# Interleaved steps of gate, up and down in a one-layer decoder, both PSUM pools shared, two step orders rewritten

## The chip, the cores and the metric

The kernel runs on one core of one Trainium2 chip. A time is the device time of one execution in microseconds (us); the median of several runs is given, and one execution was taken with the hardware profiler. The engines are named as in the profile: PE (TensorE, matrix products), PEld (its weight loads), DVE (VectorE), ACT (ScalarE), POOL (GpSimd) and SP (the queue that issues most transfers).

## What is computed

One inference step of a one-layer decoder on 1024 prompt tokens and 32 sample tokens (8 sequences of 4), 1056 tokens in all, width 1024. The layer has a combined input projection that feeds four head groups (sliding-window attention, a gated linear recurrence, a short convolution and a pooling mixer), an output projection, cross-attention into 256 memory tokens and a SwiGLU feed-forward part of hidden width 2816, each followed by a layer norm. Cut to the part that matters:

```python
mix = jnp.concatenate([o_a, o_b, o_c, o_d], axis=-1) @ w_o
x = layer_norm(ALPHA * x + mix, ln1_g, ln1_b)
x = layer_norm(ALPHA * x + memory_attention(x, mem_k, mem_v, w_xq, w_xo), ln2_g, ln2_b)
ffn = (jax.nn.silu(x @ w_gate) * (x @ w_up)) @ w_down
x = layer_norm(ALPHA * x + ffn, ln3_g, ln3_b)
```

## The kernel before

Everything is 32-bit. A matrix product in full accuracy is made of three: each operand is split into a rounded high part and a rest (`split`, line 202: a cast on ACT, line 203, and a subtraction, line 211, mostly on DVE), and `mm3` (line 194) adds high by high (line 196), high by rest (197) and rest by high (199).

PSUM has eight banks, in two pools: `PM` (line 139, tag `pm`) has three and `PSB` (line 143, tag `psb`) has five. Before, the products of the big projections, of gate and of up take `PM`; the second product of the feed-forward part, transposes and small products take `PSB`.

The work is written as Python generators, each of which stops at every `yield`; a string with one letter for each step says in which order the generators are resumed (`play`, line 1018; when the string ends, all generators are run out). A letter whose generator has ended does nothing. `ORDER1` (line 36) orders the first part: input norm (I), values (V), memory (M), columns of the input projection (T), window attention (S), the two recurrences (A, B), pooling (P). `ORDER2` (line 37) orders the second: splits of the mixed heads by token chunk (X), output projection (W), norms (N, nine steps each, in the order of `NORMS`), one cross-attention line for each of four token chunks (0 to 3, beginning with two steps of the query projection) and the first pairs of the feed-forward part (F). `ORDER3` is not used before; the order of the last part stands in `CFG`.

What is written is a preference: the library (`schedule_with_timeline_sim=True`, line 1847) settles at build time in which order each engine takes its instructions, and places the semaphores. Each engine then works through its own fixed queue.

The feed-forward part has 22 tiles of 128 hidden columns, taken in pairs p. The first pairs (p below 4) run in the second part and just behind it (`ff_early`). The rest runs in two halves of the tokens (`hf` 0: tokens 0 to 511; `hf` 1: 512 to 1055). For each pair there are three steps. `half_gate` and `half_up` (1669, 1681) call `products` (1623): it loads two weight tiles, makes sums and differences of their quarters (`sc`, `s4`, lines 1634 to 1637, in the tile `work`), splits them, and runs seven products of 12 matmuls each instead of eight, a scheme after Strassen and Winograd; the results are added up by DVE (lines 1649, 1673, 1697). Gate ends with silu; up multiplies by it (1698) and splits the product into `hh` (lines 1693 and 1694). `half_down` (1708) is the second product: it loads two weight tiles, splits them, and runs 16 steps of 6 matmuls, each of which DVE adds to the running sum `M` (1727; 1725 in the first pair of the second half).

The loop of the first half (1786) writes gate of pair p, down of pair p-1, up of pair p, each whole. The loop of the second half (1802) does the same, with one half of `finish` (1738: output norm of a block of 128 tokens, transposed by PE at line 217, then DVE, ACT, POOL and a store) after gate and one after down; there are four such blocks. In the last pair down of p-1 follows up of p. At the very end `play` runs the last down with the five remaining `finish`.

Of the kernel before, what the change touches and what calls it, by code (L numbers as in the profile page):

```python
# [19 lines left out]
KD = D // P  # L20
# [6 lines left out]
NF = DFF // P  # L27
# [5 lines left out]
LEVELS = (32, 16, 8, 4)  # L33
CFG = {'early': [[0, [0]], [0, [1]], [1, [0, 1]], [2, [0, 1]]], 'fin': {0: 0, 1: 1, 2: 1, 3: 1, 6: 1, 7: 1, 8: 1, 4: 0}, 'fpm': 1, 'VG': 'VVV', 'acc': 'VVV', 'xl': 'VVVV', 'mul': 'VVVV', 'zs': 'VVV', 'ai': 0, 'px': 'V', 'wo': [[0], [1], [2], [3]], 'ls': 384, 'rs': 3, 'sub': 'VVVV', 'sq2': 99, 'dn': 0, 'early2': [[3, [0, 1]]], 'order3': 'dddddddd87dddd8877dddd56dddddddd5566'}
NORMS = [(0, 2), (1, 2), (0, 4), (2, 2), (1, 4), (3, 2), (2, 4), (3, 4)]
ORDER1 = "MMIMMIIIIIVIVIIVCMMIIIVIIVVTIMTVVVTTTTTTTSTSTSTSTSTSTTTTSSAAASAATTAAAATTTTTAAAAAAATATTSSASSTTTTTTBBTTBBBBABBTTTTTTBBBBTTTBBBBBBBBTTTTTBBBTTBTTBPTBBBTTBTTPT"
ORDER2 = "XXWXXWWWWWWWNWXNWWWNNWNXWNNNWNWN00XW00NWNNWWNNN0NN0WWW0WW00W00WNWN1NNN1W11NNNNWWW1NWW11NNNFF11NNNNFF1N1N22NNNNNN22NNFFNNFNF2FFN2NF22N2NFNFN223NNFN33F3N33FNFNFFNF3N333FN3FF3F33F3F33333333FFFFNNFNNFNNFNNNFNF"
ORDER3 = "aaPPPPPPPPPPPPPPPPPPPPPPPPPbaabbbAAAAAvdvddvvdBBBBCCCCBCwccwwccxwxDDDxxDDxyEExyEEEzz"

# [49 lines left out]
def build(ctx: ExitStack, tc: tile.TileContext, A):  # L89
# [139 lines left out]
    flags = set()  # L229
# [787 lines left out]

    def play(order, streams):
        order = order.replace(" ", "")

        for a in order:
            run(streams[a], 1)
        for g in streams.values():
            run(g, 999)

# [516 lines left out]
    need("n4.0", "n4.256", "n4.512", "n4.768")  # L1542

# [75 lines left out]
    g3t = []  # L1621

    def products(hf, src, p, result):
# [17 lines left out]
        g4 = split(s4, w4[:, 0], w4[:, 1], V)  # L1641

        def prod(w, k0, x):
            ps = PM(n)
            mm3(ps, lambda k: w[0][:, k0 + k, :], lambda k: w[1][:, k0 + k, :], x[0], x[1], 4)
            return ps

        def add(o, ps, y):
            V.tensor_tensor(o, ps, y, ALU.add)

        S.copy(sn[:, 0], prod(g1, 0, B11))
        result(0, prod(g1, 4, B21), sn[:, 0], sn[:, 2])
# [52 lines left out]

    hx = {}

    def half_down(hf, p, order=None):
# [8 lines left out]
        flat = [tuple(t.rearrange("p c n -> p (c n)") for t in x) for x in hs]  # L1717
        for f, (t0, t1) in order or [(f, r) for f in range(KD) for r in PART[hf]]:
            ps = PSB()[:, :t1 - t0]
            fs = slice(f * P, f * P + P)  # L1720
            mm3(ps, lambda k: d[k][0][:, fs], lambda k: d[k][1][:, fs], lambda k: flat[k][0][:, t0 - o:t1 - o],
                lambda k: flat[k][1][:, t0 - o:t1 - o], 2)
            z = M[:, f, t0:t1]
            if hf and not p:
                V.scalar_tensor_tensor(z, z, ALPHA, ps, ALU.mult, ALU.add)
            else:
                V.tensor_tensor(z, z, ps, ALU.add)  # L1727
            yield
# [47 lines left out]

    NP = NF // 2
    tk = []
    EA = max(p for p, _ in CFG["early2"]) + 1
    t1 = sums_a(tk)  # L1780
# [70 lines left out]
```

## Time and profile before

| | us |
|---|---|
| median of 3 runs | 1448.58 |
| lowest, highest run | 1447.52, 1449.3 |
| the profiled execution's own time | 1450.38 |
| its span, first to last instruction | 1448.6 |
| PE busy in it (matmuls) | 1350.5 (93%) |
| DVE busy | 1084.1 (75%) |
| ACT busy | 656.7 (45%) |
| POOL busy | 239.6 (17%) |

The profile comes from the execution of 1450.38 us. A row of instructions gives start, length, engine, line, operation, the tile written and the tiles read (buffer numbers left out), and in square brackets how long the engine was idle before it and what ended that. PE's matmuls are pipelined: one of 256 columns is shown with 0.28 us, while the next starts some 0.12 us later. Waits are given as engine, line waiting, what it waited for, us in total, times, longest. In a table by stretch, each engine has its busy time and the number of its instructions, and PEclk is the granted clock of PE as a share of full speed.

### The profile page before, as it was taken

The numbers are of one execution on the slowest core, as the hardware profiler recorded it, in microseconds if no ns is written. First come the engines' busy times: TensorE is split into PE (matmuls) and PEld (weight loads), VectorE is DVE, ScalarE is ACT, GpSimd is POOL, SyncE is SP. The second block draws the span as 40 slices with busy tenths as digits, with TensorE's granted clock in tenths as the row PEclk, the third lists the DMA queues.
The fourth block names the chain that finished last, engine by engine and source line by source line (L and its number), as shares of the span: only waits on it lengthen the run. The fifth ranks groups of instructions, "written<-read, shape, count | busy, mean of one in ns | idle before, by whom it ended". The sixth has DMA issues, their size and how long they took to land.

```text
span 1448.6 us, 25150 instructions
## 1 busy us (share of the span) xinstructions
PE 1350.5 (93%) x10065; PEld 1279.5 (88%) x10065; DVE 1084.1 (75%) x1972; ACT 656.7 (45%) x1134; POOL 239.6 (17%) x164
## 2 busy tenths in 40 slices
PE   6999999998998997689988999999998999999995
PEld 5998888996897996589788999999998989999995
DVE  5814569588657768686575989988599988888877
ACT  4424662432655767575455434343343444333341
POOL 4322453365000001012042000000400000000001
PEclk8999999999898999699999999999999999999998
DMA  8201102111253435152411333332233333232321
GB/s 297 69 24 44 31 15 63 47 39 34 79 150 113 135 114 146 30 144 91 144 59 59 102 117 88 102 103 88 74 110 109 114 90 118 88 102 81 95 88 62
DMA packets 188446, 132.61 MB, mean 92 GB/s; under 512 B 14572, under 2 KB 177617, under 8 KB 188305
## 3 DMA queue, kind: packets, MB, share of 16 engines
q1 hardware_dynamic: 187225, 128.27, 29.6%
q0 software_dynamic: 928, 2.67, 0.6%
q8 instruction: 79, 1.29, 0.4%
q14 instruction: 38, 0.31, 0.1%
q10 hardware_dynamic: 176, 0.07, 0.0%
HBM read 125.32 MB, written 6.78 MB: 91 GB/s over the span
## 4 chain that ended last, share of the span: by engine, by line
PE 67%; DVE 17%; ACT 7%; DMA 4%; issue 3%; SPq 1%; POOL 1%; DVEq 0%; ACTq 0%; POOLq 0%
PE pm L196 14%; PE pm L197 14%; PE pm L199 14%; PE ps L196 5%; PE ps L199 5%; PE ps L197 5%; DVE wl L211 3%; PE ps L217 2%; ACT M L157 2%; ACT wh L203 1%; DMA rw<-in_w_down 1%; DMA rw<-in_w_up 1%; DVE R L458 1%; PE ps L625 1%; PE pm L1072 1%
## 5 line engine op out<-in xcount | busy, mean ns | idle before, releaser
L196 PE MATMUL pm<-Xh,wh 128*128 128x256 f32 (+3 forms) x1240 | 350.3, 306 | 20.9 <-ACT Xh L1130 6.3
L197 PE MATMUL pm<-Xl,wh 128*128 128x256 f32 (+3 forms) x1240 | 347.9, 304 | 2.3 <-DVE Xl L948 1.5
L196 PEld LDWEIGHTS pm<-Xh,wh 128*128 128x128 f32 x1240 | 238.3, 193 | 30.2 <-ACT Xh L1130 9.6
L197 PEld LDWEIGHTS pm<-Xl,wh 128*128 128x128 f32 x1240 | 238.4, 192 | 6.1 <-DVE Xl L1131 2.0
L203 ACT CAST wh<-rw 128x1024 fp32r<-128x1024 f32 x145 | 151.9, 1050 | 132.1 <-PE pm L197 77.8
L199 PE MATMUL pm<-Xh,wl 128*128 128x256 f32 (+3 forms) x1240 | 206.8, 299 | 2.2 <-DVE wl L211 2.2
L199 PEld LDWEIGHTS pm<-Xh,wl 128*128 128x128 f32 x1240 | 179.7, 189 | 4.3 <-DVE wl L211 2.6
L211 DVE TENSOR_TENSOR wl<-rw,wh 128x1024 fp32r<-128x1024 f32 x122 | 155.0, 1273 | 33.9 <-ACT wh L203 29.4
L197 PE MATMUL ps<-hh,dh 128*128 128x272 f32 (+3 forms) x592 | 152.5, 285 | 1.6 <-DVE hh L1694 1.6
L196 PE MATMUL ps<-hh,dh 128*128 128x272 f32 (+3 forms) x592 | 144.8, 287 | 5.1 <-ACT hh L1693 4.8
L1727 DVE TENSOR_TENSOR M<-M,ps 128x272 f32<-128x272 f32 (+3 forms) x280 | 107.2, 415 | 28.9 <-PE ps L199 28.0
L199 PE MATMUL ps<-hh,dl 128*128 128x272 f32 (+3 forms) x592 | 118.6, 284 | 0.0
L196 PEld LDWEIGHTS ps<-hh,dh 128*128 128x128 f32 x592 | 105.4, 189 | 7.0 <-ACT hh L1693 6.1
L197 PEld LDWEIGHTS ps<-hh,dh 128*128 128x128 f32 x592 | 108.8, 189 | 2.7 <-DVE hh L1694 2.7
L211 POOL TENSOR_TENSOR wl<-rw,wh 128x1024 fp32r<-128x1024 f32 x23 | 58.2, 2530 | 292.7 <-ACT wh L203 273.4
L199 PEld LDWEIGHTS ps<-hh,dl 128*128 128x128 f32 x592 | 92.0, 188 | 0.0
L203 ACT CAST dh<-rw 128x1024 fp32r<-128x1024 f32 x44 | 45.5, 1050 | 101.2 <-PE ps L197 45.6
L203 ACT CAST g<-work 128x1024 fp32r<-128x1024 f32 x34 | 35.6, 1048 | 72.0 <-PE pm L197 48.5
L196 PE MATMUL pm<-mixh,wh 128*128 128x256 f32 (+1 forms) x256 | 66.0, 292 | 0.0
L197 PE MATMUL pm<-mixl,wh 128*128 128x256 f32 (+1 forms) x256 | 65.6, 290 | 0.2 <-DVE mixl L1165 0.2
L196 PE MATMUL pm<-Xh,g 128*128 128x272 f32 (+1 forms) x216 | 56.7, 291 | 4.7 <-ACT g L203 3.0
L211 POOL TENSOR_TENSOR dl<-rw,dh 128x1024 fp32r<-128x1024 f32 x8 | 19.7, 2458 | 244.3 <-PE ps L217 200.8
(437 smaller groups left out, 3045.6 us busy)
## 6 DMA issues: line engine op xcount, KB each, us to landing
rw<-in_w_gate SPq DMA_DIRECT2D x45, 512.0 KB
rw<-in_w_up SPq DMA_DIRECT2D x44, 512.0 KB
rw<-in_w_down SPq DMA_DIRECT2D x44, 512.0 KB
rw<-in_w_o SPq DMA_DIRECT2D x23, 384.0 KB
rw<-in_w_in SPq DMA_DIRECT2D x15, 512.0 KB
xraw<-in_x_prompt SPq DMA_DIRECT2D x8, 512.0 KB
out_y_prompt<-y SPq DMA_DIRECT2D x8, 512.0 KB
vreg<-in_w_o SPq DMA_DIRECT2D x9, 384.0 KB
```

The source lines that it names most:

```text
L157: i = S.activation(out, in_, func, **kw)
L196: PE.matmul(out, wh(k), xh(k), start=(start and k == 0), stop=False)
L197: PE.matmul(out, wh(k), xl(k), start=False, stop=False)
L199: i = PE.matmul(out, wl(k), xh(k), start=False, stop=(k == nk - 1))
L203: S.copy(hi, raw)
L211: (e or G).tensor_tensor(lo, raw, hi.bitcast(F32), ALU.subtract)
L217: PE.transpose(out, in_, ident[:n, :n])
L458: V.tensor_tensor(r5, g5[:, :, :, 1, :], q5[:, :, :, 1, :], ALU.mult)
L625: PE.matmul(ps[:, g * 256:g * 256 + nk], M[js, g, q0:q0 + P], kT[js, k0:k0 + nk], start=True, stop=True)
L1072: PE.matmul(ps, identr, x[:, f, t0:t1], start=first, stop=False)
L1727: V.tensor_tensor(z, z, ps, ALU.add)
```

## The change

`products` now stops (`yield`) before the first product and after nearly every product, and takes its bank from either pool after the pattern MBMBMBB (M for `PM`, B for `PSB`). `half_down` stops once its weights are loaded and split, and takes its banks after the pattern BMBBMBBM. Both loops of the feed-forward part call `play` with a string for each pair: `ORDER4` for the first half, `ORDER5` for the second with `finish` as f, which is not run out at the end of a pair (the new argument `keep`), and `ORDER6` for the last pairs. `half_up` asserts at build time that down of the pair before has been written. `ORDER1` and `ORDER2` are other strings with the same letters. The former `order3` of `CFG` is now `ORDER3`, with one more d in front for the new stop.

The words that came with the change also say that the weight sums of gate get own buffers. The diff has no such edit: `sc` and `s4` stay in `work`.

```diff
-ORDER1 = "MMIMMIIIIIVIVIIVCMMIIIVIIVVTIMTVVVTTTTTTTSTSTSTSTSTSTTTTSSAAASAATTAAAATTTTTAAAAAAATATTSSASSTTTTTTBBTTBBBBABBTTTTTTBBBBTTTBBBBBBBBTTTTTBBBTTBTTBPTBBBTTBTTPT"
-ORDER2 = "XXWXXWWWWWWWNWXNWWWNNWNXWNNNWNWN00XW00NWNNWWNNN0NN0WWW0WW00W00WNWN1NNN1W11NNNNWWW1NWW11NNNFF11NNNNFF1N1N22NNNNNN22NNFFNNFNF2FFN2NF22N2NFNFN223NNFN33F3N33FNFNFFNF3N333FN3FF3F33F3F33333333FFFFNNFNNFNNFNNNFNF"
+ORDER1 = "MIMMIIIMIIVIVIIIVCMMIMIVVVTTIIIVVVTTTTTTTSTSSTTSTSTSTTTTSAAASSATATAAAATTTTTAAAATAAATATSSASTTTTTTSBBTTTBBTTABBBBBBBTTTBTTTBBBBTBBBBBBBBTTTTPTTTTBBBBBPTTTTTT"
+ORDER2 = "XXWWXXWWXWWWWWNNWWWNNWNXNNNWNWWN00NXNNNNW0WWW0NWN00WW0WW00W00WNNWN1NNN1W11NNNWWW1NNF1F1NNN11NNNNF1WW1FNNNNNNNN2222NNFF22NNNNFNNF2FF2FN2FFNN2F233NN3FNF33FNFFNFN33N3N3F3N3F3FF33F33F33333FN3F3FFFNFFFFNNNNNNNN"
+ORDER3 = "ddddddddd87dddd8877dddd56dddddddd5566"
+ORDER4 = "gggdggddggddggddddddddddddduuuuuuuuu"
+ORDER5 = "gggdggddggddggddddfddddddddduuuufuuuuu"
+ORDER6 = "gggggggggduuuuuuuuuddddddddddddddddd"
...
         def prod(w, k0, x):
-            ps = PM(n)
+            ps = PM(n) if next(turn) == "M" else PSB()[:, :n]
...
+        yield
         S.copy(sn[:, 0], prod(g1, 0, B11))
+        yield
         result(0, prod(g1, 4, B21), sn[:, 0], sn[:, 2])
+        yield
         ps = prod(g3, 4, T2)
         add(sn[:, 0], ps, sn[:, 0])
         yield
         ps = prod(g2, 0, T3)
         add(sn[:, 1], ps, sn[:, 0])
+        yield
         ps = prod(g3, 0, T1)
         add(sn[:, 0], ps, sn[:, 0])
         result(3, ps, sn[:, 1], sn[:, 2])
+        yield
         result(1, prod(g4, 0, B22), sn[:, 0], sn[:, 0])
+        yield
         result(2, prod(g2, 4, T4), sn[:, 1], sn[:, 1])
         yield
...
-        for f, (t0, t1) in order or [(f, r) for f in range(KD) for r in PART[hf]]:
-            ps = PSB()[:, :t1 - t0]
+        yield
+        for i, (f, (t0, t1)) in enumerate(order or [(f, r) for f in range(KD) for r in PART[hf]]):
+            ps = PM(t1 - t0) if "BMBBMBBM"[i % 8] == "M" else PSB()[:, :t1 - t0]
...
     for p in range(EA, NP):
-        run(half_gate(0, p), 99)
-        if p > EA:
-            run(half_down(0, p - 1), 99)
-        run(half_up(0, p), 99)
+        play(ORDER4, {"g": half_gate(0, p), "d": half_down(0, p - 1) if p > EA else none(), "u": half_up(0, p)})
...
-    for p in range(1, NP):
-        run(half_gate(1, p), 99)
-        run(fa, 1)
-        if p < NP - 1:
-            run(half_down(1, p - 1), 99)
-        run(fa, 1)
-        if p == 5:
+    for p in range(1, NP - 1):
+        play(ORDER5, {"g": half_gate(1, p), "d": half_down(1, p - 1), "f": fa, "u": half_up(1, p)}, "f")
+        if p == 4:
             run(fa, 99)
             free(*gbs)
-        run(half_up(1, p), 99)
-        if p == NP - 1:
-            free(*g3t)
-            run(half_down(1, p - 1), 99)
+    play(ORDER6, {"g": half_gate(1, p + 1), "u": half_up(1, p + 1), "d": half_down(1, p)})
+    free(*g3t)
```

## Rows read from the trace of the kernel before

**Rows 1.** The page's slices: PE's busy tenths in 40 equal parts.

```profile
PE   6999999998998997689988999999998999999995
```

**Rows 2.** Busy time by stage: stretch, length, engines with counts, granted clock, DMA.

```profile
0.00:390.00 390.00, 366.78 (x2310) 331.64 (x2311) 245.22 (x440) 162.92 (x323) 150.13 (x110) 0.96 0.23 69
390.00:825.00 435.00, 393.10 (x2992) 363.23 (x2991) 309.19 (x515) 255.57 (x497) 53.70 (x32) 0.95 0.36 105
825.00:1020.00 195.00, 191.80 (x1615) 190.67 (x1615) 170.08 (x327) 74.98 (x96) 2.51 (x1) 1.00 0.34 100
1020.00:1060.00 40.00, 36.98 (x287) 36.77 (x286) 25.45 (x34) 17.62 (x28) 17.63 (x13) 0.96 0.30 91
1060.00:1200.00 140.00, 130.69 (x1031) 128.30 (x1031) 125.71 (x251) 59.68 (x76) 6.44 (x4) 1.00 0.34 104
1200.00:1400.00 200.00, 198.07 (x1572) 197.03 (x1572) 171.21 (x317) 78.22 (x98) 1.08 (x1) 1.00 0.32 96
```

**Rows 3.** The timeline of PE near 852 us.

```profile
851.65 0.40 PE L199 MATMUL ps<-hh,dl 128*128 128x256 f32 x2
851.88 0.28 PE L197 MATMUL pm<-tl,g 128*128 128x256 f32 x1
...
852.12 0.28 PE L196 MATMUL ps<-hh,dh 128*128 128x256 f32 x1
```

**Rows 4.** Waits of PE from 825 to 1020 us: total, times, longest.

```profile
PE ps L196 <- ACT hh L1693: 3.0, 4, 0.9
```

**Rows 5.** Waits of PE from 1020 to 1200 us.

```profile
PE pm L196 <- DVE work L1697: 3.5, 4, 1.3
PE pm L196 <- ACT g L203: 3.0, 1, 3.0
PE pm L196 <- DVE work L1649: 2.3, 1, 2.3
PE ps L196 <- ACT hh L1693: 1.8, 2, 1.1
PE ps L197 <- DVE hh L1694: 0.7, 2, 0.5
```

**Rows 6.** Waits of PE from 1200 to 1400 us.

```profile
PE ps L197 <- DVE hh L1694: 0.8, 1, 0.8
```

**Rows 7.** The timeline of PE from 1092.5 to 1107 us.

```profile
1092.52 1.04 PE L217 MATMUL ps<-cf,M 128*128 128x128 f32 x8
...
1097.40 0.39 PE L196 MATMUL pm<-Xh,wh 128*128 128x272 f32 x1 [2.35 <-DVE work L1649]
...
1106.96 0.39 PE L196 MATMUL ps<-hh,dh 128*128 128x272 f32 x1 [0.73 <-ACT hh L1693]
```

**Rows 8.** The timeline of DVE ahead of the second of them.

```profile
1095.20 1.20 DVE L211 TENSOR_TENSOR dl<-rw,dh 128x1024 fp32r<-128x1024 f32 x1
...
1096.93 0.42 DVE L1649 TENSOR_TENSOR work<-pm,work 128x272 f32<-128x272 f32 x1
```

**Rows 9.** Waits of PE from 1400 us to the end.

```profile
PE pm L217 <- DVE y L1754: 3.1, 2, 1.8
```

**Rows 10.** Busy time of two stretches, with the columns of rows 2.

```profile
585.00:600.00 15.00, 4.00 (x17) 2.28 (x16) 9.04 (x17) 5.86 (x12) 0.00 (x0) 0.60 0.18 53
600.00:612.00 12.00, 11.63 (x45) 9.18 (x46) 5.81 (x11) 6.54 (x18) 0.00 (x0) 0.51 0.00 0
```

**Rows 11.** The timeline of PE in the same place.

```profile
592.23 1.19 PE L1121 MATMUL ps<-vreg,cf 128*128 128x256 f32 x2 [6.43 <-DVE vreg L1118]
...
600.09 0.79 PE L196 MATMUL pm<-Xh,wh 128*128 128x256 f32 x2 [4.66 <-ACT Xh L1130]
```

**Rows 12.** The timeline of ACT ahead of it.

```profile
588.72 1.04 ACT L203 CAST wh<-rw 128x1024 fp32r<-128x1024 f32 x1 [1.98 <-DMA rw<-in_w_up]
```

**Rows 13.** Waits of PE from 390 to 800 us.

```profile
PE ps L1099 <- DVE vreg L1089: 5.9, 1, 5.9
```

**Rows 14.** Busy time of the stretch 350 to 375 us, with the columns of rows 2.

```profile
350.00:375.00 25.00, 21.64 (x115) 16.27 (x114) 17.20 (x36) 7.04 (x13) 6.85 (x4) 0.66 0.30 80
```

More of the change, by code (lines that the diff above doesn't have):

```diff
@@ L33 @@
 LEVELS = (32, 16, 8, 4)
-CFG = {'early': [[0, [0]], [0, [1]], [1, [0, 1]], [2, [0, 1]]], 'fin': {0: 0, 1: 1, 2: 1, 3: 1, 6: 1, 7: 1, 8: 1, 4: 0}, 'fpm': 1, 'VG': 'VVV', 'acc': 'VVV', 'xl': 'VVVV', 'mul': 'VVVV', 'zs': 'VVV', 'ai': 0, 'px': 'V', 'wo': [[0], [1], [2], [3]], 'ls': 384, 'rs': 3, 'sub': 'VVVV', 'sq2': 99, 'dn': 0, 'early2': [[3, [0, 1]]], 'order3': 'dddddddd87dddd8877dddd56dddddddd5566'}
+CFG = {'early': [[0, [0]], [0, [1]], [1, [0, 1]], [2, [0, 1]]], 'fin': {0: 0, 1: 1, 2: 1, 3: 1, 6: 1, 7: 1, 8: 1, 4: 0}, 'fpm': 1, 'VG': 'VVV', 'acc': 'VVV', 'xl': 'VVVV', 'mul': 'VVVV', 'zs': 'VVV', 'ai': 0, 'px': 'V', 'wo': [[0], [1], [2], [3]], 'ls': 384, 'rs': 3, 'sub': 'VVVV', 'sq2': 99, 'dn': 0, 'early2': [[3, [0, 1]]]}
 NORMS = [(0, 2), (1, 2), (0, 4), (2, 2), (1, 4), (3, 2), (2, 4), (3, 4)]
-ORDER1 = "MMIMMIIIIIVIVIIVCMMIIIVIIVVTIMTVVVTTTTTTTSTSTSTSTSTSTTTTSSAAASAATTAAAATTTTTAAAAAAATATTSSASSTTTTTTBBTTBBBBABBTTTTTTBBBBTTTBBBBBBBBTTTTTBBBTTBTTBPTBBBTTBTTPT"
-ORDER2 = "XXWXXWWWWWWWNWXNWWWNNWNXWNNNWNWN00XW00NWNNWWNNN0NN0WWW0WW00W00WNWN1NNN1W11NNNNWWW1NWW11NNNFF11NNNNFF1N1N22NNNNNN22NNFFNNFNF2FFN2NF22N2NFNFN223NNFN33F3N33FNFNFFNF3N333FN3FF3F33F3F33333333FFFFNNFNNFNNFNNNFNF"
-ORDER3 = "aaPPPPPPPPPPPPPPPPPPPPPPPPPbaabbbAAAAAvdvddvvdBBBBCCCCBCwccwwccxwxDDDxxDDxyEExyEEEzz"
+ORDER1 = "MIMMIIIMIIVIVIIIVCMMIMIVVVTTIIIVVVTTTTTTTSTSSTTSTSTSTTTTSAAASSATATAAAATTTTTAAAATAAATATSSASTTTTTTSBBTTTBBTTABBBBBBBTTTBTTTBBBBTBBBBBBBBTTTTPTTTTBBBBBPTTTTTT"
[4 more added lines that the diff above has]
+ORDER6 = "gggggggggduuuuuuuuuddddddddddddddddd"
 AQ, AK, AV, BQ, BF, BI, BG, CB, CC, CHC, DV = 0, 256, 384, 512, 768, 1024, 1280, 1536, 1792, 2048, 2304
@@ L1016, in chain, with play @@
             yield from g
-    def play(order, streams):
+    def play(order, streams, keep=""):
         order = order.replace(" ", "")
@@ L1022, in play @@
             run(streams[a], 1)
-        for g in streams.values():
-            run(g, 999)
+        for a, g in streams.items():
+            run(g, 0 if a in keep else 999)
     mask01 = M[:, 6, :]
@@ L1542, in build @@
     need("n4.0", "n4.256", "n4.512", "n4.768")
+    NP = NF // 2
+    EA = max(p for p, _ in CFG["early2"]) + 1
     raw3.clear()
@@ L1641, in products @@
         g4 = split(s4, w4[:, 0], w4[:, 1], V)
+        turn = iter("MBMBMBB")
         def prod(w, k0, x):
-            ps = PM(n)
+            ps = PM(n) if next(turn) == "M" else PSB()[:, :n]
             mm3(ps, lambda k: w[0][:, k0 + k, :], lambda k: w[1][:, k0 + k, :], x[0], x[1], 4)
@@ L1681, in half_up @@
     def half_up(hf, p):
+        if p - 1 in downs[hf]:
+            need(f"d{hf}.{p - 1}")
         sl = sil_of(hf)
@@ L1706, in build @@
     hx = {}
+    downs = (range(EA, NP - 1), range(0, NP - 2))
     def half_down(hf, p, order=None):
@@ L1729, in half_down @@
         free(*tiles, *[t for pair in d for t in pair])
+        flags.add(f"d{hf}.{p}")
     gbt = [None]
@@ L1775, in finish @@
         yield
-    NP = NF // 2
     tk = []
-    EA = max(p for p, _ in CFG["early2"]) + 1
     t1 = sums_a(tk)
@@ L1785, in build @@
     g3t.extend(H([P, KD, P], F32R, s="g3") for _ in range(2))
+    none = lambda: iter(())
     for p in range(EA, NP):
-        run(half_gate(0, p), 99)
-        if p > EA:
-            run(half_down(0, p - 1), 99)
-        run(half_up(0, p), 99)
+        play(ORDER4, {"g": half_gate(0, p), "d": half_down(0, p - 1) if p > EA else none(), "u": half_up(0, p)})
     free(*tk)
@@ L1817, in build @@
     dn = half_down(1, NP - 1, [(f, r) for r in ((784, T), (640, 784), (512, 640)) for f in range(KD)])
-    play(CFG["order3"], {"d": dn, **{str(i): finish(i) for i in (4, 5, 6, 7, 8)}})
+    play(ORDER3, {"d": dn, **{str(i): finish(i) for i in (4, 5, 6, 7, 8)}})
 _INS = ["x_prompt", "x_sample", "cache_swa_k", "cache_swa_v", "state_hgrn", "state_conv", "state_pool",
```

## The prediction

> **What bounds the kernel now.** I read the page's slices first [rows 1]: TensorE (PE) is at nine tenths or more in most of the span. Then the table by stage [rows 2], with the granted clock beside the busy time. Three things are to be seen there. In the first half of the feed-forward part (825 to 1020 us) PE is busy 191.80 of 195 us, so 3.2 us are idle. In the second half it loses 3.0 us at the turn (1020 to 1060), 9.3 us while the first four output blocks are normalised beside it (1060 to 1200) and 1.9 us after that (1200 to 1400): 17.4 us from 825 to 1400. The two parts before it, input projection with the mixers (0 to 390) and output projection with cross-attention (390 to 825), are idle for 23.2 and 41.9 us, at a mean clock of 0.96 and 0.95. The change adds and removes no matmul, no copy and no transfer. It moves steps, so its whole effect is waits of PE that go and waits that come.
>
> Third, the order in which steps are written is not the order in which PE runs them. At 851.65 PE runs the second product (`ps<-hh,dl`), at 851.88 two matmuls of a gate product (`pm<-tl,g`), at 852.12 the second product again [rows 3], though lines 1787 to 1790 write the whole gate ahead of the whole second product. The library settles each engine's queue when the kernel is built, from the written order as a preference and from its own idea of what is ready. So the interleaving that the new strings spell out is partly there already, and what they add is less than it looks.
>
> **The change part by part.** All terms are us against the profiled execution, 1450.38, whose span is 1448.6. The median of the runs shown is 1448.58, so I take 1.8 off at the end.
>
> *PSUM banks.* Before, the seven products of gate and of up have three banks (`pm`) and the second product five (`psb`). After, four of seven products take `psb` and six of sixteen steps of the second product take `pm`. A pair then asks each `pm` bank 12/3 = 4 times instead of 14/3 = 4.7, and each `psb` bank 18/5 = 3.6 times instead of 16/5 = 3.2. A step of the second product on a `pm` bank can now wait for a product's bank, with everything that PE has behind it. The waits that this can take away are those of a product's first matmul for an addition on VectorE (DVE) that empties a bank: 3.5 and 2.3 us, all in 1020 to 1200 [rows 5], 5.8 in sum. One is seen whole: PE stops 2.35 us at 1097.40 for line 1649 [rows 7], which DVE ran at 1096.93 because work that nothing waited for, a 1.20 us subtraction of a weight of the second product among it, stood ahead of it [rows 8]. With more banks PE would have gone on. But DVE is busy 125.71 of 140 us there [rows 2], and its work stays the same, so part of the lead is given back at the next thing that it must deliver. I take -4. Bounds: -5.8, and 0 if all is given back. The Trainium skill, "Perfetto Trace Analysis", section Matmuls, says that independent groups of matmuls should rotate through different PSUM banks so that emptying one overlaps the next. By that rule alone this term would be the full -5.8 and the forecast 1.8 lower; the row of DVE's load is why I don't follow it that far.
>
> *Finer steps and their order.* Gate now stops after each product, and two products of the next gate and the loading of the second product's weights are written ahead of the first step of the second product. The waits aimed at are those of the second product for `hh`, cast by ScalarE (ACT) or subtracted by DVE at the end of up: 3.0 us in four waits [rows 4], 1.8 and 0.7 [rows 5], 0.8 [rows 6], together 6.3; the longest of them are about 1 us. Two products are 24 matmuls of about 0.12 us (191.80 us over 1615 matmuls [rows 2]), 2.9 us, enough to cover any one. Since the queue already mixes the streams [rows 3], I take -4. Bounds: -6.3, and on the other side a wait of 0.75 us (the mean of [rows 4]) at every one of the 15 pairs that has such a turn, 11.3, so +5.
>
> *What is moved with them.* On SP's queue the loads of a pair stay in the order gate, second product, up, so nothing there is passed; the same holds for the last pair, where gate, up, second product was the order before. POOL's part is the additions of the output norm, which stay two halves per pair. Moving these halves behind eight steps of the second product, and into up, costs nothing as long as products and steps cover it; uncovered, the eight transposes of a block are 1.04 us [rows 7], so 0 to +4 for four blocks, and I take 0. The new condition ahead of up is checked when the kernel is built and is no wait on the chip. The wait of 3.0 us for `g` at the turn [rows 5] has the same steps ahead of it before and after: 0.
>
> *The end.* The last second product now takes `pm` banks in 9 of its 24 steps, while the last five norms take two `pm` banks each. PE already waits 3.1 us there for the reading of a `pm` bank, line 1754 [rows 9]. I take +1; bounds 0 and +3.1 for the same wait once more.
>
> *ORDER2.* Most letters move by one or two places; some letters at the ends ask a stream that has already ended, and do nothing. Two moves meet long waits. (a) The steps 2 to 7 of the norm of tokens 256 to 511 now stand ahead of the query projection of tokens 512 to 767, before behind it. In that place PE waits 6.43 us at 592.23 for this norm [rows 11], then stays at half clock: 0.60 of full in 585 to 600 and 0.51 in 600 to 612 [rows 10]. In the norm's way stood ACT, which at 588.72 had waited 1.98 us for a weight and then cast it for 1.04 us [rows 12], 3.0 together. If that goes, -3, and with it a share of the half-clock cost of 12 x (1 - 0.51) = 5.9 us in proportion to the hole: 3/11.1 of it (6.43 and the 4.66 us that follow it in [rows 11]), -1.6. (b) One split of the third token chunk moves from place 14 to 8. It is now out of the way of the sum on which the 5.9 us wait of line 1099 hangs [rows 13]; by the length of a 128x1024 cast (1.04 us [rows 12]) and as much on DVE, an estimate, -2. Together -6.6. Bounds: the whole of (a), 6.4 + 4.7 + 5.9 = -17, with (b), -5.9, makes -23; a new hole like the first of (a) with its half clock, 6.4 + 5.9, makes +12.
>
> *ORDER1.* Small shifts among the recurrences and projections. The nearest place is 350 to 375 us, 21.64 busy of 25 at a clock of 0.66 [rows 14]: 3.4 idle, and 25 x 0.34 = 8.5 by the clock. Nothing in the string adds work there with certainty, so -1. Bounds: -12 and, by one more such idle stretch without its clock, +3.4.
>
> Sum: -4 - 4 + 0 + 1 - 6.6 - 1 = -14.6; 1450.38 - 14.6 = 1435.8 as profiled, 1434.0 as a median. I say 1435.
>
> **The rivals.** *The queue does it already.* If the library's mixing [rows 3] has taken what interleaving can give, and DVE sets the pace of 1060 to 1200, the two feed-forward terms shrink to -2 and the two strings give nothing: 1448.6 - 2 + 1 = 1448. For it: rows 3, and 198.07 busy of 200 us in 1200 to 1400 [rows 2], where there is nothing to gain. Against it: the waits of [rows 5] have names that the change touches.
>
> *Not what it says.* The words speak of own buffers for the weight sums of gate; the diff has no such buffer, `sc` and `s4` stay in `work`. That part can give nothing, and I count none; if the rest gives nothing either, the time is the 1448 of the case above, and it is counted there.
>
> *Slower: a late operand at the head of PE's queue.* Place: the 15 pairs in which steps of the second product are now written between products. If the build believes `hh` or a bank to be ready sooner than it is, the step holds everything behind it: at 1106.96 PE waited 0.73 us for `hh` with other work of the next gate still undone [rows 7]. Price per pair: one such wait of 0.75 and one bank wait of 1 (5.8 us over the five waits counted in [rows 5] is 1.2), 1.75; over 15 pairs 26, less the 12.1 that these two kinds cost today, +14. With +1 for the end and nothing from the strings: 1463. It decides from the seventh pair on (7 x 1.75 = 12). For it: the trace shows the build to be wrong about `hh` in nine places [rows 4 to 6]. Against it: 1200 to 1400 runs nearly without waits under the same build. The Trainium skill, "TensorE: Matmul & The Clock Gate", section The mechanism, states that matmuls start and end strictly in program order; the row at 1106.96 agrees, with 0.73 us.
>
> *Larger gain.* The long holes of ORDER2 and ORDER1 close: 1448.6 - 23 - 12 - 7, about 1410 with most of it.
>
> **How the numbers follow.** Chances: the forecast 0.50 (its own range 1424 to 1445), the queue does it already 0.20, slower 0.23, larger gain 0.07. A measurement of this kernel can tell about 0.2% from no change, 2.9 us; of the 0.20 I put 0.07 just beyond that line. Faster: 0.50 + 0.07 + 0.07 = 0.64; same 0.13; slower 0.23. The range must take in most of the slower case and some of the larger gain: 1415 to 1458.
>
> **What would show it.** In the waits of PE, lines 1697 and 1649 should be gone between 1020 and 1200 and `hh` waits should be under 3 us in all; if DVE's busy share in 1060 to 1200 goes to 95% and the waits are only renamed, the second case holds. The hole before line 1121 near 585 us should be under 4 us, and line 1099's near 448 us under 4. The stages should end earlier by about 1 (input), 7 (attention) and 7 (feed-forward) us. I am wrong if a new wait of several us stands in ORDER2's part, or if the 15 pairs each show a wait of a second-product step.

## The result, and the profile after

The median went from 1448.94 us (four runs, 1447.52 to 1449.55) to 1431.24 us (four runs, 1428.38 to 1431.89): a ratio of 0.9875, with a 95% interval from 0.9858 to 0.9893. The forecast was 1435, and the range 1415 to 1458 holds the result. The sum was right, but not its parts: the strings brought more than twice what I gave them, and the feed-forward edit, for which I had counted 7 us, brought nothing.

The profiled execution took 1430.61 us with a span of 1428.8. First its table by stage, with the columns of [rows 2]; the stretches are moved so that each begins and ends near the same work as there.

```profile
0.00:386.00 386.00, 366.36 (x2313) 331.83 (x2314) 242.98 (x441) 161.56 (x323) 147.09 (x110) 0.96 0.23 68
386.00:803.00 417.00, 385.80 (x2991) 358.21 (x2990) 304.03 (x512) 254.50 (x497) 52.99 (x32) 0.98 0.37 110
803.00:996.00 193.00, 191.82 (x1622) 191.42 (x1621) 169.82 (x329) 74.13 (x97) 2.51 (x1) 1.00 0.34 104
996.00:1036.00 40.00, 32.88 (x250) 32.49 (x249) 26.04 (x35) 16.88 (x27) 17.90 (x13) 0.91 0.32 100
1036.00:1176.00 140.00, 136.64 (x1078) 135.73 (x1077) 126.54 (x245) 62.20 (x78) 4.81 (x2) 0.99 0.33 100
1176.00:1376.00 200.00, 196.55 (x1560) 195.58 (x1559) 173.56 (x322) 80.23 (x103) 2.92 (x1) 1.00 0.32 96
1376.00:1429.00 53.00, 35.53 (x264) 33.91 (x262) 34.63 (x91) 20.52 (x26) 8.15 (x5) 0.81 0.18 63
```

Against [rows 2]: the input part is 4 us shorter and the second part 18 us shorter for the same number of matmuls. The 140 us beside the output norm have 136.64 busy instead of 130.69. But the turn has 32.88 instead of 36.98, and its clock fell from 0.96 to 0.91. A few marks in PE's timeline make it a sum, in us from the start of the span. The first three are the starts of the first matmul of their kind; both columns come from one execution each:

| | before | after | gained up to there |
|---|---|---|---|
| first matmul of the output projection | 397.7 | 393.4 | 4.3 |
| first product of the pairs behind the early ones | 808.9 | 784.5 | 24.4 |
| first matmul of 272 columns (second half) | 1021.0 | 995.9 | 25.1 |
| end of the span | 1448.6 | 1428.8 | 19.8 |

So 24.4 us had been gained when the feed-forward loops began, and 4.6 of them were lost again in what the interleaving rewrote. The waits of PE tell where. From 996 to 1200 us after, to be held against [rows 5]:

```profile
PE ps L199 <- ACT dh L206: 7.1, 1, 7.1
PE ps L199 <- ACT hh L1708: 4.8, 2, 2.4
PE ps L199 <- DVE work L1686: 1.1, 1, 1.1
PE ps L199 <- DVE M L1744: 0.6, 1, 0.6
```

The waits for a product's bank, 3.5 and 2.3 us before, are gone, as the banks term said (their lines are 1712 and 1656 now); 1.1 us for the addition at the end of gate (line 1686, 0.6 us before at 1673) are left. In their place stand one wait of 7.1 us for `dh`, a cast weight of the second product, at the turn, and 4.8 us for `hh`, which was 1.8. From 1376 us to the end, against [rows 9]:

```profile
PE pm L220 <- DVE y L1772: 2.6, 1, 2.6
PE pm L199 <- DVE y L1772: 2.3, 1, 2.3
PE pm L199 <- DVE M L1744: 1.3, 1, 1.3
PE ps L199 <- ACT dh L206: 1.0, 1, 1.0
```

The second and the third are steps of the last second product (`L199`) that wait for a `pm` bank. And ACT shows there what no row of before had, its timeline in the tail:

```profile
1366.44 0.66 ACT L160 ACTIVATE work<-work 128x544 f32<-128x544 f32 x1 [2.40 <-DVE work L1686]
1367.12 1.28 ACT L156 ACT_TABLE_LOAD   x1
1368.40 1.28 ACT L160 ACT_TABLE_LOAD   x1
1369.70 0.66 ACT L160 ACTIVATE work<-work 128x544 f32<-128x544 f32 x1
...
1418.68 1.28 ACT L159 ACT_TABLE_LOAD   x1
1421.46 0.20 ACT L159 ACTIVATE fag<-fag 128x1 f32<-128x1 f32 x1 [1.50 <-DVE fag L224]
1421.68 1.28 ACT L159 ACT_TABLE_LOAD   x1
1422.98 0.20 ACT L159 ACTIVATE fag<-fag 128x1 f32<-128x1 f32 x1
```

The kernel loads the table with Ln and Exp once (line 156), behind the silu that was written last. Here the last gate's two silus had changed places in the queue: one ran behind that load (1369.70) and brought its own table, and from then on each Ln and each Exp of the output norm (line 159) got a load of its own: ten between 1387.9 and 1421.7 us. DVE waits for the last Exp:

```profile
1421.29 0.14 DVE L224 TENSOR_SCALAR fag<-fag 128x1 f32<-128x1 f32 x1
1423.21 0.16 DVE L227 TENSOR_TENSOR fag<-fag 128x1 f32<-128x1 f32 x1 [1.78 <-ACT fag L159]
```

### The profile page after: what moved, and what is told of

The parts are those of the page before. It is cut to its first block, busy times and chain, and to the rows that moved or that the text cites. A ratio compares the mean times of both kernels' runs of the same rounds, so it can differ in the third digit from the quotient of the medians.

```text
span 1428.8 us, 25133 instructions
## 1 busy us (share of the span) xinstructions
PE 1345.6 (94%) x10065; PEld 1279.2 (90%) x10065; DVE 1077.6 (75%) x1972; ACT 670.0 (47%) x1147; POOL 236.4 (17%) x164
## 4 chain that ended last, share of the span: by engine, by line
PE 41%; DVE 7%; DMA 4%; ACT 3%; issue 2%; POOL 0%; DVEq 0%; ACTq 0%; POOLq 0%; SPq 0%
PE ps L199 7%; PE ps L202 7%; PE ps L200 7%; PE pm L199 6%; PE pm L200 6%; PE pm L202 6%; DMA rw<-in_w_gate 2%; DVE wl L214 1%; DMA rw<-in_w_up 1%; PE ps L1313 1%; ACT L159 1%; ACT dh L206 1%; DMA rw<-in_w_down 0%; PE ps L1358 0%; DVE M L1481 0%
## 5 line engine op out<-in xcount | busy, mean ns | idle before, releaser
L199 PE MATMUL pm<-Xh,wh 128*128 128x256 f32 (+3 forms) x944 | 270.6, 310 | 14.7 <-ACT Xh L1133 9.8
L200 PE MATMUL pm<-Xl,wh 128*128 128x256 f32 (+3 forms) x944 | 267.2, 306 | 3.4 <-DVE Xl L1134 1.9
L199 PEld LDWEIGHTS pm<-Xh,wh 128*128 128x128 f32 x944 | 180.8, 192 | 21.5 <-ACT Xh L1133 11.4
L200 PEld LDWEIGHTS pm<-Xl,wh 128*128 128x128 f32 x944 | 180.7, 192 | 7.2 <-issue 2.5
L202 PE MATMUL pm<-Xh,wl 128*128 128x256 f32 (+3 forms) x944 | 159.4, 305 | 0.0
L199 PE MATMUL ps<-hh,dh 128*128 128x272 f32 (+3 forms) x370 | 99.9, 291 | 15.3 <-ACT dh L206 8.1
L200 PE MATMUL ps<-hh,dh 128*128 128x272 f32 (+3 forms) x370 | 99.1, 286 | 0.0
L199 PEld LDWEIGHTS ps<-hh,dh 128*128 128x128 f32 x370 | 70.2, 191 | 17.4 <-ACT dh L206 8.6
L199 PE MATMUL ps<-Xh,wh 128*128 128x272 f32 (+1 forms) x296 | 76.5, 287 | 0.0
L200 PE MATMUL ps<-Xl,wh 128*128 128x272 f32 (+1 forms) x296 | 76.4, 287 | 0.0
L200 PEld LDWEIGHTS ps<-hh,dh 128*128 128x128 f32 x370 | 70.2, 190 | 0.4 <-DVE hh L1709 0.4
L199 PE MATMUL pm<-mixh,wh 128*128 128x256 f32 (+1 forms) x256 | 65.9, 291 | 0.2 <-ACT mixh L160 0.2
L199 PE MATMUL pm<-hh,dh 128*128 128x272 f32 (+3 forms) x222 | 60.8, 291 | 3.8 <-DVE y L1772 2.3
```

Of the source, the lines that this page charges most:

```text
L199: PE.matmul(out, wh(k), xh(k), start=(start and k == 0), stop=False)
L200: PE.matmul(out, wh(k), xl(k), start=False, stop=False)
L202: i = PE.matmul(out, wl(k), xh(k), start=False, stop=(k == nk - 1))
```

## The experiments

Each kernel was timed beside the kernel before on the same chip. Times are medians; "of 1450" turns a ratio's interval into us, with 1450 for the kernel before. The experiments were timed in three groups, each with its own runs of the kernel before (medians 1450.75, 1449.64 and 1450.33). Where kernels of different groups are compared, the difference of their ratios is given too; it is good to about 4 us.

**The strings and the feed-forward edit apart.** Theory: the gain lies in the strings. Rival: in the interleaving, as my sum had it by half. Four kernels: before with one new string, before with both (`o12_only`, the two edits together), and the changed kernel with both strings of before (`ffn_only`).

```diff
-ORDER1 = "MMIMMIIIIIVIVIIVCMMIIIVIIVVTIMTVVVTTTTTTTSTSTSTSTSTSTTTTSSAAASAATTAAAATTTTTAAAAAAATATTSSASSTTTTTTBBTTBBBBABBTTTTTTBBBBTTTBBBBBBBBTTTTTBBBTTBTTBPTBBBTTBTTPT"
+ORDER1 = "MIMMIIIMIIVIVIIIVCMMIMIVVVTTIIIVVVTTTTTTTSTSSTTSTSTSTTTTSAAASSATATAAAATTTTTAAAATAAATATSSASTTTTTTSBBTTTBBTTABBBBBBBTTTBTTTBBBBTBBBBBBBBTTTTPTTTTBBBBBPTTTTTT"
```

> The kernel before with the new ORDER1 alone. By the milestones of the two traces (the first output projection begins at 397.7 us before and at 393.4 after) it should give about -4 us, 1444 to 1446, if the stages add up. By the prediction's own sum it gives -1. If the parts only work together, it gives nothing or a loss.

```diff
-ORDER2 = "XXWXXWWWWWWWNWXNWWWNNWNXWNNNWNWN00XW00NWNNWWNNN0NN0WWW0WW00W00WNWN1NNN1W11NNNNWWW1NWW11NNNFF11NNNNFF1N1N22NNNNNN22NNFFNNFNF2FFN2NF22N2NFNFN223NNFN33F3N33FNFNFFNF3N333FN3FF3F33F3F33333333FFFFNNFNNFNNFNNNFNF"
+ORDER2 = "XXWWXXWWXWWWWWNNWWWNNWNXNNNWNWWN00NXNNNNW0WWW0NWN00WW0WW00W00WNNWN1NNN1W11NNNWWW1NNF1F1NNN11NNNNF1WW1FNNNNNNNN2222NNFF22NNNNFNNF2FF2FN2FFNN2F233NN3FNF33FNFFNFN33N3N3F3N3F3FF33F33F33333FN3F3FFFNFFFFNNNNNNNN"
```

> The kernel before with the new ORDER2 alone. By the milestones (the last early second product ends at 813.7 us before and at 791.5 after, 18 us more gained than at the end of the first part) it should give about -18 us, near 1431. By the prediction's sum it gives -6.6, near 1442. If the gain hangs on what ORDER1 leaves behind (free buffers, clock), clearly less than 18.

> Both new strings ORDER1 and ORDER2, the feed-forward part as before. If the strings carry the gain, about -22 us, near 1427, faster than the changed kernel. By the prediction's sum -7.6, near 1441.

> The change of the feed-forward part alone (steps, strings 3 to 6, shared banks), both old strings ORDER1 and ORDER2. By the milestones it is a loss of about 2 to 5 us (the end of the kernel comes 4 us later after the last product of 272 columns), 1450 to 1454. By the prediction's sum it is a gain of 7, near 1442.

| kernel | median us | ratio, 95% | of 1450 |
|---|---|---|---|
| new ORDER1 alone | 1450.59 | 0.9996, 0.9984 to 1.0009 | -2 to +1 |
| new ORDER2 alone | 1440.01 | 0.9925, 0.9911 to 0.9938 | -13 to -9 |
| both strings | 1431.59 | 0.9864, 0.9848 to 0.9880 | -22 to -17 |
| feed-forward edit alone | 1452.51 | 1.0015, 1.0003 to 1.0028 | 0 to +4 |
| the change | 1431.24 | 0.9875, 0.9858 to 0.9893 | -21 to -16 |

The strings carry the whole gain. They don't add up: ORDER1 is worth nothing beside the old ORDER2 and 8.4 us beside the new one. In the trace it does end the input part earlier everywhere: the output projection begins at 397.4 to 399.2 us in the three profiles with the old ORDER1 and at 391.7 to 396.6 in the eleven with the new one. With the old ORDER2 the second part gives this back: from that mark to the first product of the later pairs it takes 411.1 us before, 413.3 with ORDER1 alone, 400.3 with ORDER2 alone and 392.6 with both. These are single executions; the one of ORDER2 alone was its slowest and the one of both its fastest, so they overstate the last step.

**Which letters of ORDER2.** Theory: move (a) of the prediction. Rivals: everything up to the place of (a), or the late letters. Both kernels have the new ORDER1.

```diff
-ORDER2 = "XXWXXWWWWWWWNWXNWWWNNWNXWNNNWNWN00XW00NWNNWWNNN0NN0WWW0WW00W00WNWN1NNN1W11NNNNWWW1NWW11NNNFF11NNNNFF1N1N22NNNNNN22NNFFNNFNF2FFN2NF22N2NFNFN223NNFN33F3N33FNFNFFNF3N333FN3FF3F33F3F33333333FFFFNNFNNFNNFNNNFNF"
+ORDER2 = "XXWXXWWWWWWWNWXNWWWNNWNXWNNNWNWN00XW00NWNNWWNNN0NN0WWW0WW00W00WNWN1NNN1W11NNNNWWW1NWW11NNNFF11NNNNFF1N1NNNNNNN2222NNFFNNFNF2FFN2NF22N2NFNFN223NNFN33F3N33FNFNFFNF3N333FN3FF3F33F3F33333333FFFFNNFNNFNNFNNNFNF"
```

> The kernel before with the new ORDER1, and of the new ORDER2 move (a) alone: the steps 2 to 7 of the norm of tokens 256 to 511 are written ahead of the query projection of tokens 512 to 767. The new ORDER1 alone made 1450.6, both strings 1431.6. If (a) carries the gain, as the prediction's largest single step would have it, 1431 to 1437. By the prediction's own size for (a), -4.6, 1446. If the gain is the sum of many small moves, or lies in the late letters, 1448 to 1451.

Measured: 1451.04 us, ratio 1.0006 (0.9993 to 1.0019). Move (a) alone is worth nothing. Its place in the trace shows why, the waits of PE from 560 to 612 us in this kernel:

```profile
PE ps L1121 <- DVE vreg L1118: 8.2, 2, 7.1
PE pm L196 <- ACT Xh L1130: 5.0, 2, 4.7
```

Before, they were 7.5 (longest 6.4) and 5.0 us: the hole of [rows 11] stayed as it was. (The profiled execution, 1443.79 us, was the shortest of this kernel; the median is used for its time.)

The other kernel has the first 125 letters of the new string, and behind them those of the old in their order:

```diff
-ORDER2 = "XXWXXWWWWWWWNWXNWWWNNWNXWNNNWNWN00XW00NWNNWWNNN0NN0WWW0WW00W00WNWN1NNN1W11NNNNWWW1NWW11NNNFF11NNNNFF1N1N22NNNNNN22NNFFNNFNF2FFN2NF22N2NFNFN223NNFN33F3N33FNFNFFNF3N333FN3FF3F33F3F33333333FFFFNNFNNFNNFNNNFNF"
+ORDER2 = "XXWWXXWWXWWWWWNNWWWNNWNXNNNWNWWN00NXNNNNW0WWW0NWN00WW0WW00W00WNNWN1NNN1W11NNNWWW1NNF1F1NNN11NNNNF1WW1FNNNNNNNN2222NNFF22NNNNFFFFNF22N2NFNFN223NNFN33F3N33FNFNFFNF3N333FN3FF3F33F3F33333333FFFFNNFNNFNNFNNNFNF"
```

> The kernel before with the new ORDER1 and the first 125 letters of the new ORDER2, moves (a) and (b) among them; the rest of the letters in the order of before. Between 386 and 600 us the kernel with both strings is about 10 us ahead of the kernel with the new ORDER1 alone, and another 10 come between 600 and 803. If the first letters carry all, 1431 to 1433. If the late letters carry what comes after 700 us (6.5 us of busy time), 1437 to 1439. If only the strings as a whole work, 1445 or more.

Measured: 1442.43 us, ratio 0.9940 (0.9923 to 0.9957), in none of the three ranges. So the first 125 letters are worth 8.2 us (from 1450.59), and the late ones 10.8 more (to 1431.59): more than I had expected of the late ones, so both halves of the string matter. The same two stretches, first with the late letters of before, then with both strings whole:

```profile
600.00:650.00 50.00, 45.11 (x347) 42.64 (x346) 35.09 (x59) 27.95 (x55) 7.66 (x4) 0.93 0.36 106
700.00:803.00 103.00, 95.04 (x725) 89.89 (x724) 74.10 (x124) 48.00 (x87) 30.55 (x17) 0.97 0.27 77
```

```profile
600.00:650.00 50.00, 47.76 (x390) 44.89 (x390) 37.69 (x62) 33.16 (x62) 8.43 (x5) 1.00 0.39 117
700.00:803.00 103.00, 100.07 (x807) 96.67 (x806) 79.44 (x129) 53.89 (x93) 28.60 (x16) 1.00 0.29 85
```

Between 700 and 803 us PE is idle 8.0 us with the old late letters and 2.9 with the new. The longest wait there is for the silu of an early pair, with the old late letters and then with the new:

```profile
PE pm L196 <- DVE sil L1432: 4.0, 1, 4.0
```

```profile
PE pm L196 <- DVE sil L1432: 1.5, 1, 1.5
```

It is 4.0 us in the kernel before too. My prediction had no row of this stretch.

**The end: tables and banks.** Theory: the loads of ACT's table. Rival: the `pm` banks of the last second product. (In kernels with the first edit, and in those further on that have it, the lines below it stand two lower than in the changed kernel.)

```diff
-        i = S.activation(out, in_, func, **kw)
+        chain = func in (AF.Sigmoid, AF.Silu) and table["set"] == "other"
+        with tc.issue_after(table["last"]) if chain else nullcontext():
+            i = S.activation(out, in_, func, **kw)
```

> The changed kernel with one addition: each silu is issued behind the silu before it, so that the last gate's second silu can't end up behind the load of the table for Ln and Exp. Theory of the tables: the ten table loads of 1.28 us each among the last five norms go, the tail after the last product of gate and up (47.1 us before, 55.2 in the changed kernel) shrinks by 2 to 6, and the time by as much: 1425 to 1429. Rival, the banks: ACT is idle enough in the tail to hide the loads, and the waits of PE there come from the last second product's `pm` banks; then the loads go and the time stays within 1 us of the changed kernel's 1431.

Measured: 1427.75 us, ratio 0.9848 (0.9828 to 0.9867). No table load is left between the two silus and the end but the kernel's own, and Ln and Exp run as one pair again:

```profile
1367.16 1.21 ACT L162 ACTIVATE work<-work 128x544 f32<-128x544 f32 x2 [2.75 <-DVE work L1688]
1368.28 0.37 ACT L1661 COPY work<-pm 128x272 f32<-128x272 f32 x1
1368.66 1.28 ACT L156 ACT_TABLE_LOAD   x1
...
1419.42 0.44 ACT L159 ACTIVATE fag<-fag 128x1 f32<-128x1 f32 x2 [3.16 <-DVE fag L226]
```

The tail, from the last matmul of gate and up to the end, is 51.5 us against 55.2 in the changed kernel. That ordering the silus removes the loads is shown. That it is worth 3.5 us rests on medians whose intervals overlap, and on this tail.

```diff
-            ps = PM(t1 - t0) if "BMBBMBBM"[i % 8] == "M" else PSB()[:, :t1 - t0]
+            ps = PM(t1 - t0) if not order and "BMBBMBBM"[i % 8] == "M" else PSB()[:, :t1 - t0]
```

> The changed kernel, but the last second product (the one that is played with the last five norms) takes all its banks from `psb`, as before the change. Theory of the banks: the waits of PE for `y` (2.6 and 2.3 us) and `M` (1.3) in the tail go, -3 to -6, 1425 to 1428. Theory of the tables: those waits only follow from norms that are late on ACT, so at most 1 us goes: 1430 to 1431. The term of the prediction for the end was +1 (0 to +3.1), which by itself would make 1430.

Measured: 1429.36 us, ratio 0.9858 (0.9837 to 0.9879), 1.9 less than the changed kernel: less than the banks theory wanted, more than the rival, and inside the uncertainty.

> Both edits together. If tables and banks are two separate costs of the end, the tail comes back to 47 us and the time is 1431 - 8 = 1423, with 1422 to 1425 as its range; below the 1431.6 of the kernel with the two strings alone by the 4.3 us that the second half of the feed-forward part gained. If both are one chain, it is no better than the better of the two single edits by more than 1 us.

Measured, with both edits: 1426.00 us, ratio 0.9837 (0.9817 to 0.9858), 5.2 less than the changed kernel, where the two single edits sum to 5.4. By the medians these are two separate costs. The tails don't bear it out: 55.2 us in the changed kernel, 51.5 with the first edit, 54.3 with the second, 51.3 with both, so behind the table's 3.7 us the banks add 0.2. As the interval of both edits overlaps that of the first alone, a cost of the banks of its own is not shown. The time lies just above the range I had given, and the tail came back to 51.3 us, not to the 47 I had expected. Part of that is only where the mark lies: from it to the last matmul of the second product it is 33.2 us in this kernel and 29.0 before, so more of that product runs behind it.

**Banks and steps apart.** With the end as before or repaired in all four kernels, the square of the two feed-forward terms can be filled: both strings and neither (`o12_only`), steps alone, banks alone, both (`tbl_dnpsb`).

```diff
-            ps = PM(n) if next(turn) == "M" else PSB()[:, :n]
+            ps = PM(n)
...
-            ps = PM(t1 - t0) if "BMBBMBBM"[i % 8] == "M" else PSB()[:, :t1 - t0]
+            ps = PSB()[:, :t1 - t0]
```

> Both edits, and the banks of the products and the second product all as before the change (products on `pm`, second product on `psb`); the finer steps and the strings of the feed-forward part stay. It parts the two feed-forward terms of the prediction. If the banks carry the 4.3 us that the second half gained, its stretch from the first 272-column matmul to the last of gate and up goes back from 377.8 to 382 and the time is 4 above the kernel with both edits, near 1427. If the finer steps carry them, the stretch stays at 378 and the time is equal within 1. The prediction had -4 for each.

For the banks alone, the kernel with both new strings and the loops of before:

```diff
+        turn = iter("MBMBMBB")
...
-            ps = PM(n)
+            ps = PM(n) if next(turn) == "M" else PSB()[:, :n]
...
-            ps = PSB()[:, :t1 - t0]
+            ps = PM(t1 - t0) if not order and "BMBBMBBM"[i % 8] == "M" else PSB()[:, :t1 - t0]
```

> Both new strings and the shared banks in the products and the second product (the last second product on `psb`, each silu issued behind the one before), with gate, second product and up written one after the other as before the change. With the run with finer steps and no shared banks (1435.6), the run with both (1426.0) and the run with neither (1431.6) it fills the square. If banks and steps add as two terms, 1431.6 - 5.6 - 4 = 1422; if the steps are worth nothing beside the banks, 1426; if each needs the other, 1430 or more. The prediction had -4 for the banks: 1427.6.

| median us (ratio, 95%) | steps as before | finer steps |
|---|---|---|
| banks as before | 1431.59 (0.9848 to 0.9880) | 1435.57 (0.9886 to 0.9920) |
| shared banks | 1423.67 (0.9785 to 0.9826) | 1426.00 (0.9817 to 0.9858) |

Shared banks gain 7.9 us beside the old steps and 9.6 beside the new ones (8.6 and 9.6 by the ratios). The two profiled spans with the old steps differ by less, 1426.4 and 1422.8, so the size is some 4 to 10. Finer steps cost 4.0 us beside the old banks (5.7 by the ratios); beside shared banks the 2.3 by medians lies inside the uncertainty, and the 4.6 by the ratios barely outside it. The traces point the same way. From the first matmul of 272 columns to the last of gate and up, with the columns of [rows 2], first with neither, then with finer steps, then with shared banks:

```profile
997.00:1379.00 382.00, 367.89 (x2888) 363.96 (x2887) 323.89 (x599) 155.22 (x202) 25.17 (x16) 0.99 0.32 97
1000.00:1390.00 390.00, 372.04 (x2907) 367.80 (x2906) 324.09 (x604) 153.27 (x201) 25.22 (x16) 0.99 0.31 95
998.00:1373.00 375.00, 363.24 (x2870) 362.04 (x2870) 319.51 (x594) 154.52 (x202) 25.09 (x16) 0.99 0.33 99
```

With both it is 377 us. (Of these single executions the one with neither was the fastest of its kernel and the one with finer steps the slowest, so 390 against 382 overstates.) Behind the turn, its first 40 us, PE is idle 10.9 us with neither, 14.9 with finer steps, 4.6 with shared banks and 6.5 with both. What the finer steps cost is seen in the kernel without shared banks. Its waits of PE from 1060 to 1365 us begin with

```profile
PE ps L201 <- ACT hh L1710: 11.9, 5, 4.2
```

and at the longest of them ACT's timeline reads

```profile
1079.81 1.05 ACT L208 CAST dh<-rw 128x1024 fp32r<-128x1024 f32 x1 [2.05 <-DMA rw<-in_w_down]
1086.17 1.04 ACT L208 CAST wh<-rw 128x1024 fp32r<-128x1024 f32 x1 [5.32 <-DMA rw<-in_w_up]
1087.13 0.64 ACT L1710 CAST hh<-work 128x544 fp32r<-128x544 f32 x1
```

The cast of `hh`, for which PE waits, stands on ACT behind the cast of a weight of up that is still on its way from memory. The same pair, a weight that waits for `w_up` and `hh` behind it, stands before each of the other four waits, at 1126 and 1163 us with 5.01 and 4.66 us. The pair is not new: in the kernel before it stands at 1213.97 and 1347.95 us, but there the weight waited only 1.5 and 1.3 us. Why the transfers land later with the finer steps was not tried. In the changed kernel the two longest waits for `hh`, 2.4 us each, have another source. There ACT itself waits, for DVE's multiplication at the end of up (line 1713), which ran behind subtractions of weights (line 214, at 1111.33 and 1115.65):

```profile
1117.25 0.65 ACT L1708 CAST hh<-work 128x544 fp32r<-128x544 f32 x1 [4.44 <-DVE work L1713]
```

The other, at 1191.10 us, is alike, with 4.86 us of ACT for line 1713. In the kernel with banks alone no wait for `hh` is left from 1040 us to the tail (its lines lie two to six below those of before):

```profile
PE pm L198 <- DVE M L1731: 4.2, 3, 2.3
PE pm L198 <- DVE work L1677: 0.4, 1, 0.4
```

**The turn.** The 7.1 us for `dh` are there with banks alone as well, and with finer steps alone PE waits 3.0 us for `g` as before, so the steps are not their cause. One line more on the kernel with both repairs of the end:

```diff
-            ps = PM(t1 - t0) if not order and "BMBBMBBM"[i % 8] == "M" else PSB()[:, :t1 - t0]
+            ps = PM(t1 - t0) if not order and (hf or p < NP - 1) and "BMBBMBBM"[i % 8] == "M" else PSB()[:, :t1 - t0]
```

> The kernel with both repairs of the end, and at the turn between the two halves the last second product of the first half also on `psb` alone. There PE waits 7.1 us for the second cast of the second product's weights, where before it waited 3.0 us for `g`. If the shared banks brought the second product's steps ahead of the gate's there, the 7.1 goes back to 3.0 and the time is 1426 - 4 = 1422. If the finer steps did it, the 7.1 stays and the time is 1426. The sum of the repairs would then be all that the feed-forward edit had to give.

Measured: 1423.05 us, ratio 0.9809 (0.9792 to 0.9826), 2.9 less than without the line (4.1 by the ratios, with about as much uncertainty). The wait for `dh` is gone; PE waits for `g` again, as before the change, and once for `Xl`:

```profile
1027.45 0.60 PE L201 MATMUL pm<-Xh,g 128*128 128x272 f32 x1 [4.46 <-ACT g L208]
1030.16 0.60 PE L202 MATMUL pm<-Xl,g 128*128 128x272 f32 x1 [1.21 <-DVE Xl L1613]
```

This kernel and the one with banks alone are the two fastest; their intervals lie below that of the changed kernel. Both in one, old steps and the turn on `psb`, was not tried.

## Why the prediction came out right, and where its steps failed

*Banks, -4.* Right in kind and too small: 4 to 10 us, and both medians lie beyond my bound of -5.8. The waits of lines 1697 and 1649 went as said. But the waits for `hh`, which I had set down to the finer steps, went with the banks too: with both strings alone they are 3.0 us in the first half and 3.6 behind the turn, with shared banks and the old steps there are none. What it also lacked is the turn. I wrote that the wait for `g` there has the same steps ahead of it before and after. It has not: with a `pm` bank free to it, PE's queue took the second product of the last pair ahead of the gate, and stood there 7.1 us for the second weight's cast, which ACT ran at 1028.05 behind four other casts, the first of which had waited 2.39 us for a subtraction on DVE. The run with the turn on `psb` gives 2.9 us of that back.

*Finer steps, -4.* Wrong in sign: +4 to +6 beside the old banks, between nothing and some 5 us beside the new ones. The step that failed is "enough to cover any one". Its count was off: `ORDER4` and `ORDER5` write two products ahead of the loading of the second product's weights and four ahead of its first step, and before the change all seven stood there, so the strings write less between `hh` and its use, not more. And it looked only at what PE has between the two. With the finer steps alone ACT's queue set when `hh` came: the cast of up's weight stood ahead of it and waited up to 5.3 us for its transfer. In the changed kernel DVE's queue did. Under "What is moved with them" I went through SP's queue and POOL's and left out both. The slower rival named the right mechanism, a late operand at the head of PE's queue; with finer steps alone there are five such waits behind the turn, one of 4.2 us, three of 2.1 to 2.5 and one of 1.0, not fifteen of 0.75, and the shared banks and the strings outweighed it.

*Moved halves of the output norm, 0.* No wait for a transpose appeared in 996 to 1200 us. Whether these halves make `hh` later on ACT or DVE was not tried alone.

*The end, +1.* Too small: 5.2 us by both repairs. The bank wait I had in mind is 1.9 of them by medians and 0.2 by the tails. The rest is the table, which the prediction couldn't see in [rows 9], since before the change ACT had no load there (the kernel's own ran at 1391.71). "No copy" was right and not enough: ACT runs 1147 instructions instead of 1134, and the 13 more are table loads, 37 instead of 24. It could have been seen in the code: the load is tied to one of two silus, and an edit that lets the queue swap them unties it.

*ORDER2, -6.6.* Too small, and neither named move did what I gave it. (a) alone: 1451.04, hole unchanged. (b), which was not run alone, should have shortened the 5.9 us wait of [rows 13]; it is nearly as long after, line 1102 now, from 386 to 500 us:

```profile
PE ps L1102 <- DVE vreg L1092: 5.5, 1, 5.5
```

The step that failed is reading a move of the written order as a move in the engine's queue, which the prediction itself warns of with [rows 3]. In the hole of [rows 11] the wait for `vreg` is gone after the change, but the next one, for `Xh`, grew from 4.7 to 8.5 us with 1.9 for `Xl` ahead of it; the clock behind it was 0.69 in the first 10 us, and 0.51 in 12 before [rows 10]. The larger share came from letters to which I gave no term, after 600 us. The bound of -23 did hold it.

*ORDER1, -1.* Alone 0; beside the new ORDER2 8.4. I treated the strings as two terms, and they are one. Why the second part gives the earlier start back with the old ORDER2 is not settled.

Together: -14.6 foreseen and -17.7 measured, made of about -19 for the strings (foreseen -7.6), -8 to -10 for the banks, +2 to +5 for the steps, +5 for the end (the strings against the 1450.75 of the kernel before in their own runs). The last three sum to about nothing, foreseen as -7. That the total fell within 4 us of the forecast is therefore luck: the strings gave some 11 us more than I said, for no reason that I gave, and the feed-forward part 7 us less. The second case, "the queue does it already", had the sum of the feed-forward part about right, though not its reason, and the strings wrong.

My own signs say the same. Lines 1697 and 1649 are gone, and so is the hole before line 1121 (1124 now). But `hh` has 4.8 us where I said under 3, line 1099's wait 5.5 where I said under 4, and the stages gained 4, 20 and -5 us where I said 1, 7 and 7. The wait of several us in ORDER2's part, which I had named as a sign of being wrong, is there: 8.5 us for `Xh`, 4.7 before.

## What to carry to other kernels

When steps are interleaved, follow each of them through the queue of every engine that it uses, and ask at each cast or copy whether a transfer can stand ahead of it; with the finer steps alone it was the engine that isn't busy, ACT, that held PE. Where a load of state, such as an activation table, is ordered behind one instruction, look for others of its kind that a scheduler may put behind it. Two strings of preferences for neighbouring stages are one change: time them together and apart before a size is given to either.

## What the runs showed of the hardware

A table load on ACT took 1.283 us in every case, and ten stood in the last 41 us, where before there was none. The Trainium skill, "ScalarE activation tables: per-element evaluation and per-set limits", section What a function is on this engine, states that two functions in different sets are one load of 1283 ns apart and that two functions in one set need no switch; the trace agrees with the duration. Here each Ln and each Exp got a load, although the one load of line 156 had served both until a silu's load stood behind it.

The hole at the turn cost more than itself. After 7.1 us without a matmul at the turn the granted clock was 0.50, the lower of its two levels (1.2 GHz), from 1029 to 1033 us, and 0.99 from 1033 on:

```profile
1022.00:1029.00 7.00, 0.02 (x1) 0.00 (x0) 6.23 (x7) 4.58 (x7) 4.18 (x4) 0.80 0.01 4
1029.00:1033.00 4.00, 3.86 (x18) 3.86 (x19) 4.00 (x5) 1.16 (x3) 0.00 (x0) 0.50 0.69 248
1033.00:1036.00 3.00, 3.00 (x25) 2.82 (x25) 3.00 (x8) 0.00 (x0) 0.54 (x1) 0.99 0.92 288
```

Matmuls of 256 columns started 0.21 us apart in those 4 us and 0.12 us apart ahead of the hole; for the 18 of them that makes 18 x 0.09 = 1.6 us more than the 7.1. Little of this is new: before the change the hole of 3.02 us at 1052.44 was followed by a granted clock of 0.50 too, from 1052.4 to 1055 us, in which 11 matmuls of 272 columns started 0.23 us apart instead of 0.13, 1.1 us in all.
